# One image load, cut into two DMAs at the front of a convolution kernel

## The chip, the cores and the metric

The kernel runs on one core of a Trainium2 chip. The metric is device time in microseconds (us). All runs quoted count as fast: none is more than 1.5% above the fastest run of its kernel. Small differences are judged by ratios over several rounds, with their 95% intervals.

A *packet* is one record of a DMA in the trace: one run of bytes that one of the 16 DMA engines moves. The *pitch* of the rows that a DMA reads is the distance in memory from the start of one row to the start of the next. The *table load* is the instruction with which ScalarE loads its activation table before its first copy.

## The reference

A 3x3 convolution with padding 1 over 16 images of 64 channels and 64x64 pixels, 64 output channels, plus a residual, all float32:

```python
batch, c_in, h, w, c_out, k = 16, 64, 64, 64, 64, 3
x_pad = np.pad(x, ((0, 0), (0, 0), (pad, pad), (pad, pad)))
# for all b, co, ci, kh, kw:
output[b, co] += weight[co, ci, kh, kw] * x_pad[b, ci, kh:kh+h, kw:kw+w]
return output + residual
```

Inputs, residual and output are 16.8 MB each: 50.5 MB cross the DMA queue.

## The kernel before

Two images at a time fill 128 partitions: partition = image and channel, and each row of 64x64 pixels is 16 KB (16,384 B) that lie together in x. ScalarE casts a pair to bfloat16, TensorE multiplies into PSUM, VectorE adds PSUM to the residual in place, and SyncE issues every DMA.

```python
def load_x(p):
    return nc.sync.dma_start(out=xr[p % NXR][:, :],
        in_=x_bc[128 * p : 128 * p + 128, :]).then_inc(s_x[p % NXR], 16)
...
for p in range(NPAIR):                       # SyncE's program
    if p >= NXR:
        nc.sync.wait_ge(s_half, 2 * (p - NXR) + 3)
    if p == 0:
        to_the_front(load_x(p))              # moved ahead of the opening barrier
        nc.sync.dma_start(out=wraw[:, :], in_=w_rows[:, :]).then_inc(s_w, 16)
    else:
        load_x(p)
    if p in (0, 1, 3, 5, 7):
        load_ro((p + 1) // 2)                # residual, straight into the output tile
...
for n in range(B):                           # ScalarE's program
    ...
    if im == 0:
        nc.scalar.wait_ge(s_x[p % NXR], 16 * (p // NXR + 1))
    i = nc.scalar.copy(out=t[64:128, 0:J, :], in_=x4[hp, :, 0, :])
```

`to_the_front` takes a DMA out of the kernel's block and puts it into the opening block, before SyncE arrives at the barrier at which all engines meet. The first load is therefore the first instruction of the span.

## Time and profile before

| | before |
|---|---|
| median time | 122.76 us (122.63 to 122.86, 3 runs) |
| span in the profile | 120.8 us |
| DMA queue busy | 98.5%, 418 GB/s on average |
| TensorE, VectorE, ScalarE busy | 73%, 63%, 52% |
| first packet, end of the first packets' slowness | 1.01 us, about 3.2 us |

How to read it: a compute engine that is busy 73% of the time does not set the end here. The queue does: the time is the bytes at the steady rate, plus what is lost at the start and the end. The prediction shows the lines.

One measure is used throughout. The view of a stretch gives the rate from 1 to 8 us (length, then busy time of PE, PEld, DVE, ACT and POOL with counts, granted clock, DMA share, GB/s). The kernel before:

```profile
1.00:8.00 7.00, 0.00 (x0) 0.00 (x0) 0.00 (x0) 1.45 (x2) 2.17 (x12) 1.00 1.03 372
```

At the steady 430 GB/s of its later stretches the same 7 us would have moved more; the **loss at the start** is 7 x (1 - 372/430) = 0.94 us. A packet counts where it starts, so the measure is coarse: one 16 KB packet more on each engine is 37 GB/s. The times at which loads land are finer.

### The profile page before, as it was taken

The numbers are of one execution on the slowest core, as the hardware profiler recorded it, in microseconds if no ns is written. First come the engines' busy times: TensorE is split into PE (matmuls) and PEld (weight loads), VectorE is DVE, ScalarE is ACT, GpSimd is POOL, SyncE is SP. The second block draws the span as 40 slices with busy tenths as digits, with TensorE's granted clock in tenths as the row PEclk, the third lists the DMA queues.
The fourth block names the chain that finished last, engine by engine and source line by source line (L and its number), as shares of the span: only waits on it lengthen the run. The fifth ranks groups of instructions, "written<-read, shape, count | busy, mean of one in ns | idle before, by whom it ended". The sixth has DMA issues, their size and how long they took to land.

```text
span 120.8 us, 734 instructions
## 1 busy us (share of the span) xinstructions
PE 87.9 (73%) x393; PEld 10.7 (9%) x105; DVE 76.0 (63%) x40; ACT 63.1 (52%) x37; POOL 2.4 (2%) x16
## 2 busy tenths in 40 slices
PE   0024499999999999999999999999999990000000
PEld 0011001101010011011111111011111100000000
DVE  0005400789898988989879898988989879500000
ACT  4049959948999923999960999883000000000000
POOL 5200000000000000000000000000000000000000
PEclk9999999999999999999999999999999999855555
DMA  7999999999999999999999999999999999999994
GB/s 168 428 428 428 428 428 434 428 434 434 428 434 434 434 428 434 434 434 434 434 434 423 423 428 434 423 412 434 434 434 434 423 434 434 434 428 434 434 434 174
DMA packets 3504, 50.48 MB, mean 418 GB/s; under 512 B 304, under 2 KB 432, under 8 KB 432
## 3 DMA queue, kind: packets, MB, share of 16 engines
q1 hardware_dynamic: 3504, 50.48, 98.5%
HBM read 33.70 MB, written 16.78 MB: 418 GB/s over the span
## 4 chain that ended last, share of the span: by engine, by line
PE 71%; DVEq 2%; DVE 2%; issue 0%
PE ps L87 53%; PE ps L86 18%; DVEq L130 2%; DVE ro L203 2%
## 5 line engine op out<-in xcount | busy, mean ns | idle before, releaser
L203 DVE TENSOR_TENSOR ro<-ps,ro 64x2048 f32<-64x2048 f32 x32 | 73.2, 2289 | 17.7 <-PE ps L87 17.2
L87 PE MATMUL ps<-xp,wl 128*128 128x504 bf16 (+1 forms) x288 | 80.0, 388 | 0.0
L86 PE MATMUL ps<-xp,wl 128*128 128x504 bf16 (+1 forms) x96 | 37.4, 389 | 3.4 <-PEq L224 3.4
L174 ACT CAST xp<-xr 64x2048 bf16<-64x2048 f32 x16 | 30.3, 1896 | 18.3 <-DMA xr<-in_x_dram 17.2
L178 ACT CAST xp<-xr 64x2048 bf16<-64x2048 f32 x16 | 30.4, 1897 | 0.4
L86 PEld LDWEIGHTS ps<-xp,wl 128*128 128x128 bf16 x96 | 9.5, 99 | 79.1 <-issue 79.1
L190 DVE CAST wl<-ps 32x192 bf16<-32x192 f32 x8 | 2.8, 348 | 10.6 <-PE ps L216 10.5
L216 PE MATMUL ps<-ident,wraw 128*32 128x128 f32 x9 | 2.1, 413 | 8.3 <-DMA wraw<-in_weight_dram 8.3
L216 PEld LDWEIGHTS ps<-ident,wraw 128*32 128x32 f32 x9 | 1.2, 137 | 8.7 <-issue 8.2
L174 ACT ACT_TABLE_LOAD x1 | 1.3, 1283 | 1.0 <-SPq L130 1.0
L183 ACT CAST wl<-ps 32x192 bf16<-32x192 f32 x4 | 1.2, 306 | 0.0
L162 POOL MEMSET xp<- 64x64 bf16 x4 | 0.6, 147 | 0.2
L161 POOL MEMSET xp<- 64x64 bf16 x4 | 0.6, 145 | 0.2
L150 POOL TENSOR_SCALAR_AFFINE_SELECT ident<-ident 128x128 f32<-128x128 f32 x1 | 0.3, 294 | 0.2 <-POOL ident L148 0.2
L164 POOL MEMSET wl<- 64x192 bf16 x1 | 0.3, 253 | 0.1
L163 POOL MEMSET wl<- 64x192 bf16 x1 | 0.3, 252 | 0.1
L148 POOL MEMSET ident<- 128x128 f32 x1 | 0.2, 205 | 0.6 <-SPq L130 0.6
L260 POOL MEMSET const-bfloat16-1.0<- 128x1 bf16 x1 | 0.1, 112 | 0.0
L260 POOL MEMSET const-uint8-127<- 128x1 uint8 x1 | 0.1, 112 | 0.0
L260 POOL MEMSET const-float32-0.0<- 128x1 f32 x1 | 0.1, 105 | 0.2 <-issue 0.2
L260 POOL MEMSET const-float32-1.0<- 128x1 f32 x1 | 0.1, 109 | 0.0
## 6 DMA issues: line engine op xcount, KB each, us to landing
xr<-in_x_dram SPq DMA_DIRECT2D x8, 2048.0 KB, 15.3
ro<-in_residual_dram SPq DMA_DIRECT2D x3, 4096.0 KB, 24.0
out_dram<-ro SPq DMA_DIRECT2D x3, 4096.0 KB, 33.2
ro<-in_residual_dram SPq DMA_DIRECT2D x2, 2048.0 KB, 15.9
out_dram<-ro SPq DMA_DIRECT2D x2, 2048.0 KB, 12.8
wraw<-in_weight_dram SPq DMA_DIRECT2D x1, 144.0 KB, 7.1
```

The costliest lines, as they stand in the source:

```text
L86: return e.matmul(out=out_, lhsT=lhsT, rhs=rhs, start=start, stop=stop, skip_group_check=True)
L87: return e.add_instruction(mybir.InstMatmult(name=nc.get_next_instruction_name(), engine=PE, ins=[e.lower_ap(rhs), e.lower_ap(lhsT)], outs ...
L130: with tc.tile_critical(no_gpsimd_drain=True):
L161: nc.gpsimd.memset(t[0:64, 0, :], 0.0).then_inc(s_id, 1)
L162: nc.gpsimd.memset(t[64:128, J, :], 0.0).then_inc(s_id, 1)
L174: i = nc.scalar.copy(out=t[64:128, 0:J, :], in_=x4[hp, :, 0, :])
L178: nc.scalar.copy(out=t[0:64, 1 : J + 1, :], in_=x4[hp, :, 1, :]).then_inc(s_pack, 1)
L183: i = nc.scalar.copy(**weight_block(h, *b))
L190: i = nc.vector.tensor_copy(**weight_block(h, *b))
L203: i = nc.vector.tensor_tensor(out=o4[hp, :, par, :], in0=psj[64 * par : 64 * par + 64, :, :], in1=o4[hp, :, par, :], op=ADD)
L216: i = nc.tensor.transpose(out=tp[0:32, t // 3, 128 * (t % 3) : 128 * (t % 3) + 128], in_=wraw3[:, :, t], identity=ident[:, :])
L260: nc = _bacc.Bacc("TRN2", target_bir_lowering=False, num_devices=1)
```

## The change

The first load goes as two DMAs, both in the front: the first 2 KB of each row, then the other 14 KB. Its apparent intent is to let the queue start on short packets, as the first 16 KB packets take 0.7 to 2.0 us each instead of 0.611. ScalarE waits for both.

```diff
+    X0 = NPIX // 8
...
-    def load_x(p):
-        return nc.sync.dma_start(out=xr[p % NXR][:, :], in_=x_bc[128 * p : 128 * p + 128, :]).then_inc(s_x[p % NXR], 16)
+    def load_x(p, cols=slice(0, NPIX)):
+        return nc.sync.dma_start(out=xr[p % NXR][:, cols], in_=x_bc[128 * p : 128 * p + 128, cols]).then_inc(
+            s_x[p % NXR], 16
+        )
...
-                to_the_front(load_x(p))
+                to_the_front(load_x(p, slice(0, X0)))
+                to_the_front(load_x(p, slice(X0, NPIX)))
...
-                nc.scalar.wait_ge(s_x[p % NXR], 16 * (p // NXR + 1))
+                nc.scalar.wait_ge(s_x[p % NXR], 16 * (p // NXR + 1 + (p % NXR == 0)))
```

## The prediction

> **What bounds the kernel now.** I read the page's first parts (busy shares, the 40 slices, the DMA queues), then the stretches of the first and last microseconds, then SyncE's line of time, then the waits.
>
> ```profile
> PE 87.9 (73%) x393; PEld 10.7 (9%) x105; DVE 76.0 (63%) x40; ACT 63.1 (52%) x37; POOL 2.4 (2%) x16
> ...
> DMA  7999999999999999999999999999999999999994
> GB/s 168 428 428 428 428 428 434 428 434 434 428 434 434 434 428 434 434 434 434 434 434 423 423 428 434 423 412 434 434 434 434 423 434 434 434 428 434 434 434 174
> DMA packets 3504, 50.48 MB, mean 418 GB/s; under 512 B 304, under 2 KB 432, under 8 KB 432
> ...
> q1 hardware_dynamic: 3504, 50.48, 98.5%
> ```
>
> No compute engine is above 73%, while the one DMA queue is busy for 98.5% of the span, in every slice but the first and the last, at 428 to 434 GB/s. The 50.48 MB divided by the 120.8 us span is 418 GB/s, so the span is 97% of the way to a plain copy at the steady rate: the 16 DMA engines are the bound, and the page's own chain that ended last (PE 71%) misses this, because the last stores are issued long before the queue reaches them. The packet records in the trace make it precise: nearly every packet is a whole 16 KB row that took 0.611 us, and each of the 16 engines carries 192 of them. One follows the next after about 0.607 us, so an engine needs 192 x 0.607 = 116.5 us, plus 8 weight rows at 0.047 us each (0.4 us): 116.9 us of pure moving. The rest of the 120.8 us is at the two ends.
>
> The stretches (length, busy time by engine, clock, DMA share, GB/s by the packets that started there):
>
> ```profile
> 0.00:1.00 1.00, 0.00 (x0) 0.00 (x0) 0.00 (x0) 0.04 (x1) 0.22 (x5) 1.00 0.00 0
> 1.00:2.00 1.00, 0.00 (x0) 0.00 (x0) 0.00 (x0) 1.00 (x1) 0.66 (x4) 1.00 1.62 295
> 2.00:3.00 1.00, 0.00 (x0) 0.00 (x0) 0.00 (x0) 0.24 (x1) 0.73 (x6) 1.00 0.58 213
> 3.00:4.00 1.00, 0.00 (x0) 0.00 (x0) 0.00 (x0) 0.00 (x0) 0.78 (x4) 1.00 0.90 377
> 4.00:5.00 1.00, 0.00 (x0) 0.00 (x0) 0.00 (x0) 0.00 (x0) 0.00 (x0) 1.00 1.07 459
> 5.00:8.00 3.00, 0.00 (x0) 0.00 (x0) 0.00 (x0) 0.21 (x1) 0.00 (x0) 1.00 1.01 421
> 100.00:110.00 10.00, 0.00 (x0) 0.00 (x0) 4.25 (x2) 0.00 (x0) 0.00 (x0) 0.73 1.00 428
> 110.00:119.00 9.00, 0.00 (x0) 0.00 (x0) 0.00 (x0) 0.00 (x0) 0.00 (x0) 0.50 1.01 433
> ```
>
> Nothing moves for 1.0 us. Then the queue starts badly: from 1 to 8 us the rates give 295 + 213 + 377 + 459 + 3 x 421 = 2607 KB, where the steady 430 GB/s would have moved 3010 KB. So (3010 - 2607) / 430 = 0.94 us are lost in a **slow start**. The packet records agree: all packets that start before 4 us together took 16.6 us more than 0.611 us each, 1.04 us per engine, and almost all of it lies in the first packet of an engine (0.72 to 2.03 us instead of 0.611) or the second (1.24, 1.77 and 1.35 us on three engines).
>
> SyncE's line of time:
>
> ```profile
> 0.00 0.38 SPq L72 DMA_DIRECT2D xr<-in_x_dram  x1
> 1.00 0.33 SPq L138 DMA_DIRECT2D wraw<-in_weight_dram  x1
> 1.38 0.57 SPq L77 DMA_DIRECT2D ro<-in_residual_dram  x1
> ...
> 104.58 0.98 SPq L80 DMA_DIRECT2D out_dram<-ro  x2
> ```
>
> The first load is the first instruction of the span, and its first packets start at 1.01 us, 0.63 us after the issue ended. The opening barrier lets the other engines go at 0.96 to 1.00 us. The last two stores are issued at 104.6 to 105.6 us, but the queue reaches them only when the store before them has landed, at 110.1 us in the landing records: some 4.5 us of slack.
>
> **What the Trainium skill says.** "DMA: Bandwidth & Descriptors", section "Latency and other measured facts", gives a first byte about 600 ns after a sync-issued DMA; the 0.63 us here agrees. It gives HBM access as 0.2 us on average and 2 us at high load; the slow first packets (up to 2.03 us) would fit that, but no run here yet shows that it is the cause. Section "Why small descriptors are slow (HBM only)" has a fixed overhead of a few cycles per packet. The trace agrees: a weight row of 1152 B follows the last after 0.047 us, where 1152 B at 16384 B per 0.607 us would be 0.0427 us, so a packet costs about 4 ns extra. Section "Why a DMA increments its semaphore by 16 and not by 1" warns of two DMAs in flight on one semaphore; the new wait is for 32, the full sum of both, so it is sound, and the next load into that buffer is not issued until this one has been used.
>
> **The change part by part.**
>
> 1. 128 more packets, 8 per engine, at 4 ns: 0.03 us; and one more semaphore packet per engine (9 ns in the records). Together **+0.04 us**, on the path, since the queue is the bound. Bytes are unchanged.
> 2. One more issue of 0.33 to 0.57 us (the range of SyncE's issues) ahead of the barrier. Barrier, weights issue, table load and GpSimd's fills move from 1.0 to about 1.45 us. All beside other work: the weights' rows are reached by the queue at 6.4 us and GpSimd's fills end at 3.9 us, before the transposes wait for the weights until 8.3 us. **0.**
> 3. The first packets still start at about 1.0 us, for the first issue is first as before. The second DMA's issue ends near 0.8 to 0.95 us, so its packets can start near 1.45 to 1.6 us. The 2 KB pieces hold each engine for 8 x 16384/8 B, one old packet, 0.61 us, to 1.62 us at best and later in a slow start. No hole opens. **0.**
> 4. ScalarE's first cast waits for both pieces, hence for the same last byte: 7.79 us as now. Nothing reads the 2 KB early. **0.**
> 5. The slow start itself: what is to be won is at most the **0.94 us** above. The first packet of an engine is now 2 KB (0.076 us at the steady rate), so the engines leave their common start after an eighth of the bytes, and several rows may be underway while the first is slow. If the loss belongs to long packets all starting in step, much of it goes; if it is a latency or a disturbance in time, it stays whatever the packet size. I can't tell these apart in this trace and take about a third: **-0.3 us**.
>
> Sum: +0.04 - 0.3 = -0.26, from 122.76 to **122.5 us**.
>
> **The rivals.**
>
> - *The slow start is a fixed time* (a cold memory path, or the activation table's load at 0.96 to 2.24 us, which covers the bad stretch). For it: every engine loses about once, even if in its second packet. Then only the overhead stays: 122.8 us.
> - *The crowd of long packets is the cause.* For it: two engines did their first 16 KB in 0.72 us while others took over 1.5, as if they shared something unevenly; the loss is gone once the engines are out of step, and it never comes back when loads are issued later. Then almost all 0.94 us come back: 121.9 us.
> - *The 2 KB pieces are worse*: 128 starts all 16 KB apart, in 8 rounds instead of one, make the crowding last longer. Against it: the engines are soon out of step. It could cost another 0.3 to 1 us: 123.1 to 123.8 us.
> - *The earlier front moves the compute work*: SyncE's later barrier would have to eat the slack of the last stores, 4.5 us, to be seen; a delay of 0.45 us doesn't.
>
> **Range and chances.** Runs of the kernel before lie within 122.63 to 122.86, so noise is 0.1 us. The best case is 122.76 - 0.94 + 0.04 = 121.86, the mild bad case 123.1: range **121.8 to 123.1**, predicted **122.5**. To be 2% faster the change would have to save 2.46 us, over twice all that the slow start loses: chance 0.01. To be 2% slower it would have to more than triple that loss: 0.02. Within 2%: 0.97.
>
> **What would show it.** In the changed kernel's profile: 128 + 16 more packets; two issues of SyncE before the barrier, and the weights' issue near 1.45 us instead of 1.00; first packets still near 1.0 us; a first slice with more than 168 GB/s if part 5 holds, and the same or less if a rival does; the first cast of ScalarE earlier than 7.79 us by what was saved, and the last landing earlier by the same amount, with all slices between unchanged at 428 to 434 GB/s. The prediction is wrong if the second DMA's packets leave a hole after the first's, if the first cast starts later than 8 us, or if the first DMA's start itself moves.

## The result

| | before | after |
|---|---|---|
| median time | 122.81 us (122.63 to 122.95, 4 runs) | 123.23 us (123.03 to 123.36, 4 runs) |
| ratio | 1 | 1.0034, interval 1.0013 to 1.0054 |
| span in the profile | 120.8 us | 121.5 us |
| rate from 1 to 8 us, loss at the start | 372 GB/s, 0.94 us | 336 GB/s, 1.53 us |
| first pair of images landed | 7.77 us | 8.28 us |
| second pair landed | 17.87 us | 18.38 us |
| last store landed | 119.95 us | 120.59 us |

Ratios are the mean time of one kernel's fast runs over that of the other's in the same rounds, so they are not quite ratios of the medians. The change costs 0.42 us by the medians: within 2%, but clear of the noise, in the direction opposite to the one predicted, and 0.13 us above the predicted range.

The page's slices and queue of the changed kernel:

```profile
DMA  5999999999999999999999999999999999999993
GB/s 77 439 407 432 432 432 432 432 432 432 432 432 432 432 432 432 432 432 432 432 432 432 432 432 432 432 432 432 432 432 432 432 432 432 432 432 432 432 432 162
DMA packets 3648, 50.48 MB, mean 416 GB/s; under 512 B 320, under 2 KB 448, under 8 KB 576
...
q1 hardware_dynamic: 3648, 50.48, 98.0%
```

There are 144 more packets, as predicted. Everything after the third slice runs at the steady rate; the first slice fell from 168 to 77 GB/s. The stretches of the start, in the changed kernel:

```profile
1.00:2.00 1.00, 0.00 (x0) 0.00 (x0) 0.00 (x0) 0.57 (x1) 0.30 (x2) 1.00 1.33 193
2.00:3.00 1.00, 0.00 (x0) 0.00 (x0) 0.00 (x0) 0.71 (x1) 0.78 (x5) 1.00 0.34 41
3.00:4.00 1.00, 0.00 (x0) 0.00 (x0) 0.00 (x0) 0.00 (x0) 0.73 (x5) 1.00 1.09 444
```

From 2 to 3 us the queue started packets worth 41 GB/s, where the kernel before had 213. The packet records say more: the first 2 KB packets took 0.08 to 0.28 us and most of those after them 0.084 us, but nine that start between 1.5 and 2.1 us take 1.2 to 1.5 us. Between 1.5 and 3.2 us only 11 to 14 of the 16 engines have a packet under way; in the kernel before it is nearly always all 16 from 1.3 us on. Added up, the data packets of the first 12 us took 1.12 us per engine longer than undisturbed ones, hardly more than the 1.04 us of the kernel before; what came on top, in this profile, is at least 0.42 us per engine without a packet between 1.3 and 6 us (0.01 us before). These gaps lie among the 2 KB packets: once an engine had closed its 2 KB lot, the first time at 2.74 us, its 14 KB packets followed after 0.006 us. The 0.51 us by which the first pair lands later is still there at the second pair; that is where the time was lost.

SyncE's line of time in the changed kernel, with both issues ahead of the barrier:

```profile
0.00 0.86 SPq L73 DMA_DIRECT2D xr<-in_x_dram  x2
1.47 0.33 SPq L142 DMA_DIRECT2D wraw<-in_weight_dram  x1
1.85 0.87 SPq L80 DMA_DIRECT2D ro<-in_residual_dram  x1
```

The weights' issue moved from 1.00 to 1.47 us, and ScalarE's table load from 0.96 to 1.43 us. This tempting coincidence, a barrier 0.47 us later and a loss of 0.42 to 0.51 us, was the first theory to test.

### The profile page after: what moved, and what is told of

Same layout as the page of the kernel before. It is cut to its first block, busy times and chain, and to the rows that moved or that the text cites. A ratio compares the mean times of both kernels' runs of the same rounds, so it can differ in the third digit from the quotient of the medians.

```text
span 121.5 us, 735 instructions
## 1 busy us (share of the span) xinstructions
PE 87.9 (72%) x393; PEld 10.7 (9%) x105; DVE 76.0 (63%) x40; ACT 63.1 (52%) x37; POOL 2.4 (2%) x16
## 4 chain that ended last, share of the span: by engine, by line
PE 71%; DVEq 2%; DVE 2%; issue 0%
PE ps L90 53%; PE ps L89 18%; DVEq L133 2%; DVE ro L207 2%
## 5 line engine op out<-in xcount | busy, mean ns | idle before, releaser
L178 ACT ACT_TABLE_LOAD x1 | 1.3, 1283 | 1.4 <-SPq L133 1.4
```

## The experiments

Eighteen kernels ran, each timed against the kernel before on the same chip. The losses at the start come from one profile each; what such a reading is worth is tested at the end.

### Is it the later barrier, or something that follows it?

Theory: the hold-up hangs on what follows the barrier (the table load, SyncE's next issues), so that a later barrier puts it where it costs more. Rival: the two DMAs cost by themselves.

**e1: the table load late** (kernel before).

```diff
+            if n == 0:
+                nc.scalar.wait_ge(s_id, NZERO)
             i = nc.scalar.copy(out=t[64:128, 0:J, :], in_=x4[hp, :, 0, :])
```

> The kernel before, with one edit: ScalarE waits for GpSimd's fills (done at 3.94 us) before its table load, which so moves from 0.96 us to about 4 us; the table load takes 1.28 us. Theory T (the activation table's load holds up the data packets for about a microsecond): the slow first packets go, the first 16 packets take about 0.7 us each, and long packets appear near 4 to 6 us instead; total loss unchanged, time within 0.3 us of before. Rival B (what holds the packets up comes with the opening barrier or with SyncE's later issues, not with the table): the first packets stay slow, 0.7 to 2.0 us, and nothing is slow at 4 to 6 us; time as before. Rival W (the start of the traffic itself): the same as B here.

Measured: 122.95 us, ratio 1.0006 (0.9990 to 1.0023). Its stretches:

```profile
1.00:2.00 1.00, 0.00 (x0) 0.00 (x0) 0.00 (x0) 0.00 (x0) 0.66 (x4) 1.00 1.61 295
2.00:3.00 1.00, 0.00 (x0) 0.00 (x0) 0.00 (x0) 0.00 (x0) 0.73 (x6) 1.00 0.57 197
...
4.00:5.00 1.00, 0.00 (x0) 0.00 (x0) 0.00 (x0) 0.98 (x1) 0.00 (x0) 1.00 1.03 442
```

ScalarE's 0.98 us of table load now lie between 4 and 5 us, where the queue moves 442 GB/s undisturbed, while the start is as slow as before without it. The table is not the cause of the slow start. (The Trainium skill, "ScalarE: Activation LUTs", section "What ACT_TABLE_LOAD costs", gives about 1283 ns for this instruction; the 1.28 us of the trace agree.)

**e2: the barrier late** (kernel before, with one GpSimd fill of a 128x512 scratch tensor ahead of the barrier).

```diff
                 to_the_front(load_x(p))
+                to_the_front(nc.gpsimd.memset(idle[:, :], 0.0))
```

> The kernel before, one DMA in the front as before, with one 128x512 fill by GpSimd ahead of the opening barrier, so that the barrier opens some 0.4 to 0.7 us later, as it does after the change (there 0.47 us later). Theory (the change lost its 0.4 us by opening the barrier later, and the slow start hangs on what follows the barrier): first packets of near 0.7 us, a stall that moves later by the barrier's delay, time 0.4 to 0.7 us above before. Rival (it is the second DMA or its small packets that cost): time as before, within 0.15 us, first packets as slow as before.

Measured: 122.74 us, ratio 0.9991 (0.9978 to 1.0004). The table load started at 1.37 us and the weights' issue at 1.41 us, close to the changed kernel's 1.43 and 1.47; the rate from 1 to 8 us stayed 372 GB/s. The later barrier costs nothing.

**e3: the 14 KB issued after the barrier** (changed kernel).

```diff
-                to_the_front(load_x(p, slice(X0, NPIX)))
+                load_x(p, slice(X0, NPIX))
```

> The changed kernel with the second DMA (14 KB of each row) issued after the opening barrier, ahead of the weights, so that SyncE has one issue in the front as before and the barrier opens near 0.96 us again. Barrier theory: the stall starts near 1.3 us as in the kernel before and ends by about 2.7 us; the time falls from 123.2 to between 122.6 and 122.9 us, the kernel before's. Rival (small packets or the second DMA are the cost, wherever issued): 123.1 us or more.

Measured: 123.28 us, ratio 1.0049 (1.0029 to 1.0069), although the barrier was back at the old place (table load at 0.96 us). Now the 2 KB lot landed early, at 2.86 us instead of 3.99, but a hole opened: at 2.0 us only 2 of 16 engines had a packet, for the 14 KB packets could not start before 2.02 us, and they then took up to 1.75 us each. So the time of this run can't judge the barrier: what an earlier barrier might have won, the hole could have cost. (e13, below, settles it: it has the late barrier and does not pay.) As a repair this is worth nothing. But one thing matters later: the same 128 packets of 2 KB, at the same pitch but with the 14 KB DMA issued only at 1.00 us (0.43 us in the change), took at most 0.22 us each here, and 246 of their 262 KB started in the first microsecond (193 KB in the change):

```profile
1.00:2.00 1.00, 0.00 (x0) 0.00 (x0) 0.00 (x0) 1.00 (x1) 0.66 (x4) 1.00 0.69 246
2.00:3.00 1.00, 0.00 (x0) 0.00 (x0) 0.00 (x0) 0.24 (x1) 0.73 (x6) 1.00 1.38 260
```

**e4: the table load before the barrier** (kernel before; the table's load instruction put in ScalarE's opening block).

```diff
                 to_the_front(load_x(p))
+                to_the_front(nc.scalar.add_instruction(mybir.InstLoadActFuncSet(..., act_func_set_id=0)))
```

> The kernel before with the activation table's load put ahead of ScalarE's arrival at the opening barrier, so that it starts near 0.1 us instead of 0.96; the barrier then opens near 1.9 us instead of 0.9. Theory T (the table's load holds up the packets): most of the hold-up falls before the first packet at 1.0 us, the slow start shrinks to some 0.3 us and the time falls to about 122.2 us. Rival B (what follows the barrier holds them up): packets run at full speed from 1.0 to about 2.2 us, stall until about 3.6 us, and the time rises by 0.3 to 0.6 us to about 123.2 us.

Measured: 122.90 us, ratio 1.0006 (0.9991 to 1.0021). The weights' issue went to 1.87 us, and the held-up packets started where they did before (1.0 to 2.2 us; 1.0 to 2.3 us in the kernel before). What SyncE issues later and when the engines branch does not matter either.

### Is it the length of the packets?

New theory L: long packets that reach idle engines cause the hold-up and short ones do not. Rival C: every start loses about a microsecond, whatever the packets. Rival S: a second DMA in the front costs by itself. Only the cuts of the first load change, and the semaphore's target with them:

```diff
-    X0 = NPIX // 8
+    CUTS = (0, 512, 1024, 1536, 2048, 2560, 3072, 3584, 4096)   # e5; e6, e7, e8: see their names
...
+                for a, b in zip(CUTS, CUTS[1:]):
+                    to_the_front(load_x(p, slice(a, b)))
```

> The first image load as eight DMAs of 2 KB of each row, all in the front; nothing else differs from the changed kernel. Theory L (the slow start is the first long packets: when a DMA of long packets reaches idle or lightly filled engines, many reads are asked for at once and the first packets take 1.5 us; packets of 2 KB don't do it): no hold-up while the first load runs; 0.9 us saved against the kernel before, less 56 more packets per engine than one load at 4 ns or so each plus 7 semaphore packets (0.3 us), so 122.1 to 122.4 us, provided that the change-over to 16 KB packets near 7 us is as smooth as it is in the kernel before. Rival C (a hold-up of about a microsecond falls once each engine has had its first 16 KB, whatever the packets): still a hold-up near 1.8 to 3.1 us, time 123.2 us or more.

> The first image load as four DMAs of 4 KB of each row, all in the front. Theory L: a smaller hold-up than with 16 KB packets, a quarter to a half of 0.94 us, and less overhead than with 2 KB pieces (0.15 us); 122.2 to 122.6 us. Rival C: hold-up of a microsecond as before, 123.0 us or more.

> The first image load as two DMAs of 8 KB of each row, both in the front. Theory L: hold-up of about half to all of 0.94 us, 122.4 to 122.9 us. Rival S (any second DMA in the front costs the 0.4 us that the change cost): 123.2 us. Rival C: as before, 122.8 to 123.0 us.

> The changed kernel with the order turned round: the first 14 KB of each row first, the last 2 KB second. Theory L: the long packets start from rest as in the kernel before, the hold-up is the same 0.9 to 1.0 us and only the overhead of 0.04 us is added: 122.7 to 122.95 us. Rival S (a second DMA in the front costs 0.4 us by itself, in either order): 123.1 to 123.4 us.

| first load as | time | ratio (interval) | GB/s from 1 to 8 us | loss at the start | second pair landed |
|---|---|---|---|---|---|
| e5: 8 x 2 KB | 124.50 us | 1.0134 (1.0106 to 1.0162) | 291 | 2.26 us | 19.43 us |
| e6: 4 x 4 KB | 123.31 us | 1.0031 (1.0018 to 1.0044) | 346 | 1.37 us | 18.70 us |
| e7: 2 x 8 KB | 122.93 us | 1.0007 (0.9995 to 1.0020) | 391 | 0.63 us | 17.75 us |
| e8: 14 KB, then 2 KB | 122.81 us | 0.9998 (0.9985 to 1.0011) | 370 | 0.98 us | 17.97 us |

Theory L fell: the more short packets come first, the slower. The 2 KB packets of e5 are themselves held up, all through the load: the eight lots landed 0.7 to 1.1 us apart, where 8 packets of 0.084 us are 0.67 us. Rival S fell too: e7 and e8 have two DMAs in the front like the change, and cost nothing measurable. Rival C does not hold as it stands either, as the losses run from 0.63 to 2.26 us. The overhead of a packet is too small for e5: 2 KB packets follow each other after 0.080 us where undisturbed, so 64 per engine need 5.12 us instead of 8 x 0.607 = 4.86, 0.26 us of the 1.64 us lost.

### Is it where the rows lie?

Theory A: packets that start at one common offset of a 16 KB period hinder each other at the memory, because all rows lie 16,384 B apart. Rivals: 2 KB packets are slow as such (P); only neighbouring rows help (D); the start of long packets is slow wherever they lie (C). The experiments change only the pitch of the **source** rows of the first load. They read other bytes; packets, destinations, waits and byte counts are unchanged. Their outputs are wrong, which doesn't matter for the times. With the pitch, the places that are read change too; no run reads other images at the old pitch, which would tell the two apart.

```diff
-        in_=x_bc[128 * p : 128 * p + 128, cols]
+        src = x_bc[128 * p : 128 * p + 128, cols]
+        if p == 0:   # pitch 4192 floats = 16,768 B; e9: 576 floats = 2,304 B
+            src = x.rearrange("b c h w -> (b c h w)")[0 : 128 * 4192].rearrange("(p e) -> p e", e=4192)[:, cols]
```

> Wrong on purpose (the first two images get other bytes). The eight 2 KB pieces once more, same packets, same destinations, same semaphores, but the 128 rows of a piece lie 2,304 B apart in x instead of 16,384 B. Theory A (packets that start at the same offset of a 16 KB pitch hinder each other at the memory): the eight pieces now run near the steady rate and the first image lands at 7.0 to 7.6 us instead of 9.25; time 122.3 to 122.9 us against 124.5. Rival P (2 KB packets are slow as such): lands at 9 us or later, 124.0 us or more.

> Wrong on purpose. The kernel before, the first load's rows lying 16,768 B apart in x instead of 16,384 B, so that the 16 DMA engines start at 16 different offsets of a 16 KB period; nothing else differs. Theory A: the slow start mostly goes, first packets of about 0.7 us, the first image lands near 7.0 us instead of 7.77 and the time falls by 0.5 to 0.9 us to 121.9 to 122.3 us. Rival C (a cold start of the long packets, wherever they lie): first packets 0.7 to 2.0 us as before, time within 0.15 us of before.

> Wrong on purpose. The changed kernel with that same pitch of 16,768 B for both of its first DMAs. Theory A: the hold-up of 1.8 to 3.1 us goes and the change costs only its overhead: within 0.15 us of the kernel before with the same pitch, near 122.0 to 122.4 us. Rival (the change costs by its second DMA or its packet length): still 0.4 us above the kernel before with the same pitch.

> Wrong on purpose. The eight 2 KB pieces with rows 16,768 B apart. Theory A: as the dense pieces, the first image lands at 7.0 to 7.8 us, time 122.3 to 123.0 us. Rival D (2 KB pieces need neighbouring rows, any pitch near 16 KB is slow): lands at 9 us, 124.0 us or more, while the dense pieces are fast.

| kernel, pitch of the first load's rows | time | ratio (interval) | GB/s from 1 to 8 us | loss at the start | second pair landed |
|---|---|---|---|---|---|
| e5: 8 x 2 KB, 16,384 B | 124.50 us | 1.0134 (1.0106 to 1.0162) | 291 | 2.26 us | 19.43 us |
| e9: 8 x 2 KB, 2,304 B | 123.70 us | 1.0062 (1.0048 to 1.0076) | 337 | 1.51 us | 18.33 us |
| e12: 8 x 2 KB, 16,768 B | 123.65 us | 1.0050 (1.0037 to 1.0063) | 333 | 1.58 us | 19.01 us |
| e10: before, 16,768 B | 122.80 us | 0.9984 (0.9972 to 0.9997) | 384 | 0.75 us | 17.79 us |
| e11: change, 16,768 B | 122.78 us | 0.9989 (0.9975 to 1.0004) | 379 | 0.83 us | 17.63 us |

Another pitch alone takes the whole cost away from the change: with 16,768 B the split kernel (e11) and the unsplit one (e10) take the same time. It takes away half to two thirds of the cost of the eight pieces. That is less than expected: e9 and e12 were to come down to 122.3 to 123.0 us and still took 123.70 and 123.65 us. Of the 0.6 to 0.75 us that they still pay, 0.26 us may be overhead; the rest stays open, so rival P is not wholly refuted. But e10 also shows what the pitch does not do: the first 16 KB packets of the unsplit kernel still took 0.86 to 1.73 us, and the time fell by 0.16%, not by the 0.5 us or more expected. The slow start of the kernel before is thus mostly another thing than the cost of the change.

### Which of the two DMAs, and what about the pitch?

What was still open: whether the 2 KB or the 14 KB packets pay, and whether a common offset or only this one pitch is at fault.

```diff
-        if p == 0:
+        if p == 0 and cols.start == 0:     # e13: only the 2 KB DMA;  e14: cols.start > 0, only the 14 KB DMA
...
-            ... e=4192)[:, cols]
+            ... e=8192)[:, cols]           # e15: 32,768 B, both;  e16: e=4224, 16,896 B, both
```

> Wrong on purpose. The changed kernel, the rows of only the 2 KB DMA lying 16,768 B apart. If the cost of the change is in the 2 KB pieces of one common 2 KB window of the 16 KB period: 122.7 to 122.9 us, first piece lands near 2.7 us. If it is in the common start of the 14 KB packets: 123.1 to 123.4 us, as the change.

> Wrong on purpose. The changed kernel, the rows of only the 14 KB DMA lying 16,768 B apart. If the cost is in the 2 KB pieces: 123.1 to 123.4 us. If it is in the common start of the 14 KB packets: 122.7 to 122.9 us.

> Wrong on purpose, a control. The changed kernel, the rows of both first DMAs lying 32,768 B apart: another pitch, other rows, but again all at the same offset of a 16 KB period. Theory A: the change's cost stays, 0.3 us or more above the kernel before (123.1 us or more). Rival (any other pitch or other rows would have cured it): within 0.15 us of the kernel before, as with 16,768 B.

> Wrong on purpose. The changed kernel, the rows of both first DMAs lying 16,896 B apart, 512 B more than a row, so that every row starts on a multiple of 512 B[...]. Theory A: cured as with 16,768 B, within 0.2 us of the kernel before. Rival (it was the odd alignment of 16,768 B, not the spread of the offsets): 123.1 us or more.

| pitch of the 2 KB rows, of the 14 KB rows | time | ratio (interval) | 2 KB lot landed | GB/s from 1 to 8 us | loss at the start | second pair landed |
|---|---|---|---|---|---|---|
| the change: 16,384, 16,384 | 123.23 us | 1.0034 (1.0013 to 1.0054) | 3.99 us | 336 | 1.53 us | 18.38 us |
| e14: 16,384, 16,768 | 123.23 us | 1.0037 (1.0024 to 1.0050) | 3.83 us | 352 | 1.27 us | 18.21 us |
| e13: 16,768, 16,384 | 122.65 us | 0.9984 (0.9972 to 0.9997) | 2.77 us | 377 | 0.86 us | 17.76 us |
| e15: 32,768, 32,768 | 122.86 us | 1.0000 (0.9986 to 1.0013) | 2.79 us | 393 | 0.60 us | 17.50 us |
| e16: 16,896, 16,896 | 123.00 us | 1.0012 (0.9999 to 1.0025) | 2.75 us | 396 | 0.55 us | 17.45 us |

The stretches of e13, then of e14:

```profile
1.00:2.00 1.00, 0.00 (x0) 0.00 (x0) 0.00 (x0) 0.56 (x1) 0.29 (x2) 1.00 1.03 283
2.00:3.00 1.00, 0.00 (x0) 0.00 (x0) 0.00 (x0) 0.72 (x1) 0.78 (x5) 1.00 1.16 309
```

```profile
1.00:2.00 1.00, 0.00 (x0) 0.00 (x0) 0.00 (x0) 0.56 (x1) 0.29 (x2) 1.00 1.47 219
2.00:3.00 1.00, 0.00 (x0) 0.00 (x0) 0.00 (x0) 0.72 (x1) 0.78 (x5) 1.00 0.61 158
```

The barrier and SyncE's issues up to 1.85 us are alike to 0.01 us in both, and only the source of one DMA differs. (SyncE's later issues come up to 0.48 us later in e14; in e4 they came 0.72 us later than before and cost nothing.) Moving the 2 KB rows apart removes the cost; moving the 14 KB rows does not. So **the cost of the change lies in the 2 KB packets that are read at a pitch of 16,384 B.** The pitch alone is not enough, though: in e3, with the second DMA issued 0.57 us later, the same packets were not held up and landed at 2.86 us, nearly as early as in the cured kernels. e16 shows by its early landing that it is not the odd alignment of 16,768 B; by the time alone it would not be clear, as the intervals of e16 and of the change overlap. And e15 refutes theory A in the form that I gave it: at 32,768 B all rows still share one offset of a 16 KB period, and the cost is gone. What is bad about rows of exactly 16,384 B stays open, and so does what else must come together. Packets of the same length and pitch were not held up in e3, where they come first, nor in e8, where they come last (0.08 us each). That packets suffer most while the engines are in step is thus not shown, and e3 speaks against it.

### How good is one profile, and a gain that does not arrive

e17 is the kernel before again; e18 is e16 again.

> The kernel before, unchanged, for a second profile: how far do single profiles of one kernel differ? If the readings of the start hold: 365 to 380 GB/s from 1 to 8 us, second image pair landed at 17.8 to 18.0 us, and the ratio is 1.000. If single profiles scatter by as much as the variants differ: outside of that. The hold-up of long packets at 76 to 80 us, 0.12 us in the first profile, may be anything from 0 to 0.65 us if it is chance.

> Wrong on purpose: the changed kernel with a pitch of 16,896 B, again. If its early gain is real: 385 to 400 GB/s from 1 to 8 us and the second image pair landed at 17.4 to 17.6 us, as in its first profile. If the hold-up of 0.64 us at 76 to 80 us, which gave that gain back, belongs to this kernel, it comes again and the ratio is about 1.001; if it is chance, it is smaller and differs from run to run.

| | time | ratio (interval) | GB/s from 1 to 8 us | second pair landed |
|---|---|---|---|---|
| e17: before | 122.73 us | 0.9997 (0.9970 to 1.0024) | 377 | 17.94 us |
| e18: pitch 16,896 | 123.04 us | 1.0016 (0.9991 to 1.0042) | 391 | 17.64 us |

Two profiles of one kernel differ by 5 GB/s and by 0.07 to 0.19 us of landing, not far below the smallest gap in landing between a kernel that pays and one that does not (0.23 us: 18.21 us in e14, 17.98 us in e1); for those the ratios decide, e14's 1.0037 against e13's 0.9984 in the same rounds. The early gain of e16 came again in e18: the second pair lands 0.23 to 0.49 us earlier than in the two profiles of the kernel before. But it ends no faster. From 76 to 80 us, in the last residual load, ahead of the first stores, the kernel before, then e16, then e18 (the same view):

```profile
76.00:80.00 4.00, 4.00 (x20) 0.40 (x5) 3.39 (x3) 3.19 (x3) 0.00 (x0) 1.00 1.02 426
```

```profile
76.00:80.00 4.00, 4.00 (x20) 0.49 (x5) 3.42 (x2) 3.51 (x2) 0.00 (x0) 1.00 1.00 360
```

```profile
76.00:80.00 4.00, 4.00 (x20) 0.49 (x5) 3.42 (x2) 3.63 (x2) 0.00 (x0) 1.00 1.02 393
```

There the long packets are held up once more: 0.12 us per engine in the kernel before (0.14 in e17), 0.64 in e16, 0.42 in e18, and similarly 0.70 in e15 and 0.62 in e7. The kernels with the smallest loss at the start give the gain back here, and e18 says that it is not mere chance. But an early arrival alone does not bring it about: the last image load lands at 71.32 us in e7 and at 71.31 us in e13, and e13 then loses only 0.03 us. Why is open. No variant with a right result beats the kernel before; e7 and e8 come out even. In e8 no such hold-up is seen, and e7's profile was of one of the two slowest of its six runs (123.25 us; four took 122.84 to 122.94 us), so its hold-up need not be in all of them.

## Why the prediction was wrong

- *The bound*: right. The time followed the queue: the 0.51 us by which the first pair landed later were still there at the second pair, and the slices after the third stayed at 432 GB/s. That the time stays within 2% came true as well, as it would have under every rival.
- *Part 1, overhead of 0.04 us*: not contradicted. Undisturbed, 2 KB packets follow each other after 0.080 us, as 4 ns of overhead would have it, and e8, which has the same packets in the other order, came out at 0.9998.
- *Part 2, the later barrier costs nothing*: right, shown by e2. The weights' issue came at 1.47 us, 1.45 was predicted.
- *Part 3, no hole opens*: the second DMA's descriptors came early enough, since e13 with the same issues pays nothing; and in the change each engine's 14 KB packets followed 0.006 us after the packet that closes its 2 KB lot; but some engines did stand without a packet from 1.5 to 3.2 us, among the 2 KB packets. The hole of an issue that is too late is what e3 shows.
- *Part 4, the first cast waits for the same last byte*: right in its logic; that byte came 0.51 us later, and the cast started at 8.30 instead of 7.79 us, beyond the 8 us that the prediction had named as a sign of being wrong.
- *Part 5, "the slow start itself", -0.3 us*: **the step that failed.** It took the slow start for something that shorter first packets can only shrink or leave alone. In its place, the 2 KB packets at this pitch, with the 14 KB DMA right behind them, were themselves held up: the first engine was through with them at 2.74 us, not at 1.62 us or a little later, and the loss rose from 0.94 to 1.53 us. The third rival, "The 2 KB pieces are worse", named the right suspect (starts all 16 KB apart) and a time range, 123.1 to 123.8 us, that held the result; I set it aside with "the engines are soon out of step", for which no view stood, and cut the range at its mild end. The idea of part 5 was not empty: at pitches of 32,768 and 16,896 B the split start lost only 0.60 and 0.55 us, but even there the end came no earlier.
- *The first rival, the table load*: refuted by e1 and e4. That the slow start is a fixed time of any other kind does not fit losses of 0.55 to 2.26 us.
- *The second rival, the crowd of long packets*: not borne out; in e5 and e6 the packets are shorter and the loss is larger (only with the 8 KB packets of e7 is it smaller, 0.63 us).
- *Still open*: what makes the first 16 KB packets slow in the kernel before; most of it remains with another pitch (e10, 0.75 us) and with another barrier (e2, 0.94 us).
- *Two readings of the trace before were not exact*: a fourth late packet is left out (1.11 us, from 2.30 us on), and the loss does come back later, if only by 0.12 us per engine near 78 us. Neither changes the sum.

## What to carry to other kernels

In a kernel bound by its DMA queue, equal bytes do not make a cut of a load free: look at what each packet reads and how far apart the rows lie, and compare the rate of the first slices before and after. When a loss and a shifted event have the same size, move that event alone before believing it; here the barrier moved by 0.47 us and was innocent. And follow a gain at the start to the end of the program, for it can be given back 70 us later.

## What the Trainium skill lacked or had wrong

- "DMA: Bandwidth & Descriptors", section "Latency and other measured facts", on row pitches at large powers of two: its figures are for tiles with 16 KiB rows at pitches of 512 KiB and more. Here 2 KB packets suffered at a pitch of only 16,384 B (the 2 KB lot landed at 3.99 us; at 2.69 to 2.79 us with pitches of 16,768, 16,896 and 32,768 B, and at 2.86 us at the old pitch with the next DMA issued 0.57 us later), while 8 KB pieces at 16,384 B did not (ratio 1.0007). So short packets and this smaller pitch are missing there, and so is that twice the pitch can be harmless.
- The same page, section "Why small descriptors are slow (HBM only)": the fixed overhead per packet that it tells of is seen (about 4 ns in this trace), but explains only 0.26 of the 1.64 us that eight 2 KB pieces cost.
- No page that I read has the slow start: the first 16 KB packet of an engine takes 0.7 to 2.0 us instead of 0.611, 0.86 to 0.94 us lost in the kernel before.
- No page that I read has the hold-up near 78 us, in the last residual load ahead of the first stores: 0.12 us per engine in the kernel before, 0.03 to 0.70 us in the variants named above; arrival time does not explain it (e7 and e13).
